# One wave of row loads, gated scalings as single steps, and operands three products ahead in a hybrid decoder layer

## The chip, the cores and the metric

One core of a Trainium2 chip runs the whole program. The metric is device microseconds of one execution. The kernel before took 892.74 us (median of 3 runs, 892.26 to 893.94). Engines are named as in the profile: PE is TensorE, DVE is VectorE, ACT is ScalarE, POOL is GpSimd, SP is SyncE, which issues most transfers.

## What is computed

One decoder layer on x of 1024 positions by 1024 features, then a final RMSNorm. All head groups and the gate come from one projection of the normed x; there are four heads of gated linear attention (GLA), four of HGRN2 and four of attention to a memory of 256 rows. Each head's output is normed, gated by Silu, and multiplied by the output weights.

```python
h = rms_norm(x, norm_w[layer])
proj = jnp.einsum('bsd,de->bse', h, w_in[layer])
(gq, gk, gv, glr, hq, hf, hi, xq, gate) = jnp.split(proj, split_idx, axis=-1)
...
mixed = jnp.concatenate([gla_o, hgrn_o, xo], axis=-1).astype(dtype)
mixed = mixed * jax.nn.silu(gate)
x = x + jnp.einsum('bse,ed->bsd', mixed, w_out[layer]).astype(dtype)
...
return rms_norm(x, final_norm_w)
```

## The kernel before

**Products.** Float32 products are made as three matmuls of float32r halves (`mm3`, L1520 to L1522: hi by hi, hi by lo, lo by hi). An operand is split by a cast on ACT (L176 for tiles, L1269 for weights: `whi`) and a subtraction of the cast on DVE or POOL (L177, L1270: `wlo`). The projections use a scheme of seven block products in place of eight (`pair`), whose operands A11, A12, S1, S2, S3, S4 and A22 are halves of x^T or sums and differences of them; some weight operands are differences too (L1262). x^T is stored as two halves along the sequence, of eight tiles of 128x512 each (`A` tiles).

**Weights ahead.** `w(i)` prepares operand i when it is asked for, and up to `LOOKAHEAD` (L1214) operands after it, as long as fewer than `NSLOT` = 5 are in use. A preparation is the difference (L1262), the cast (L1269) and the subtraction (L1270).

**Start.** `run` (L2120) loads the memory's operands, x^T half 1, weights, then 4 tiles of x's rows, then x^T half 2 (`load_x`). The program's own count of halves is 0 and 1; here they are first and second. The norm of the first half (`norm_x`, `first_half`) gives A12 and A11. The norm of the second half goes another way: its rows of x (positions on partitions) are squared on ACT with a running sum (`rows_factors`, L1386), the sums give four columns of factors (L1391, L212 to L217), and the columns are spread over all partitions by a matmul of ones with scaled identities (L232 on DVE, L233 on PE, into the PSUM tile `sc`). `second_half` (L1425 on) then scales the eight tiles (L1403) and builds S1 (L1432) and A22; `more_sums` builds S2, S3 and S4 (L1435, L1446). There are four `ml` buffers for the rows, so the second four loads (L1378) are issued after the fourth square.

**Groups.** Eight groups follow: two of memory attention (X0, X1), four of GLA (G0 to G3), two of HGRN2 (H0, H1), each two output tiles of 128 features. `emit` runs a group's projections unit by unit; `loop` goes over NB = 8 chunks of 128 positions: `step_A` (scores), `step_T`, `step_B` (state and output: PSUM tile `o` is copied by L1966 to an SBUF tile, five buffers, and squared by L1969), and after each chunk a share of the previous group's output units (`out_units`: weights by gated outputs into `pp`, L2017 adds a running sum that was loaded from DRAM, L2021 stores it). The output of four chunks (a half) is finished by `step_C`: `norm` computes the factors and scales all four blocks (`scale_o`, L1975 on ACT: one instruction of 128x256 per block in G, two of 128x128 in X and H), `gate(0)` and `gate(1)` each transpose four blocks (L982 on PE, PSUM tile `oT`), multiply by norm weight and gate (L987 on DVE), and split (L990 on ACT, L992 on POOL). The first half's three steps (`pend`) are taken in the loop, one after each chunk from the fifth on; the second half's (`self.tail`) between units of the next group's `emit`:

```python
if self.tail:
    if n in (0, 3, 5) or n > 5:
        self.tail.pop(0)()
```

X1 has no units of its own in `emit`, so X0's second half goes through `background` in X1's loop. H1's second half is finished among the last output units.

**Order.** Each engine runs its instructions in the order of its queue. A list scheduler sets that order for all engines from the program's order and its own durations, so a step moved in the source can move instructions of every queue.

## Time and profile before

| what | value |
|---|---|
| runs | 892.26, 892.74, 893.94 us, median 892.74 |
| profiled execution | 894.03 us, its span 892.3 us |
| PE busy | 856.6 us (96%) |
| DVE, ACT, POOL busy | 624.0 (70%), 529.0 (59%), 79.1 us (9%) |
| mean granted clock of TensorE | 0.99 of full |
| moved by DMA | 113.94 MB, mean 128 GB/s |

The span is the time from the first to the last instruction; 1.7 us of the execution lie around it. A matmul of 512 columns shows as 0.39 to 0.40 us busy, while the next one starts 0.23 us after it: they overlap, so the start to start distance is the cost of one. "idle before <- releaser" in a row is the time that the engine waited ahead of the instruction, and whose end released it.

### The profile page before, as it was taken

How to read it: one execution, taken by the hardware profiler on the slowest of the kernel's cores; microseconds unless marked ns; L12 is line 12 of the kernel's file. 1: busy time of each engine (PE TensorE's matmuls, PEld its weight loads, DVE VectorE, ACT ScalarE, POOL GpSimd, SP SyncE). 2: the span in 40 equal slices, each digit the busy share in tenths (PEclk: the TensorE clock that was granted, in tenths of full speed). 3: DMA queues.
4: the chain of work that ended last, by engine and by line, in shares of the span. 5: the costliest groups of instructions: out<-in, count | busy, mean ns of one | idle time of the engine just before them, and what ended most of it. 6: DMA issues, size and time to landing. Idle time of an engine off the chain costs nothing.

```text
span 892.3 us, 13841 instructions
## 1 busy us (share of the span) xinstructions
PE 856.6 (96%) x4734; PEld 714.9 (80%) x4734; DVE 624.0 (70%) x1504; ACT 529.0 (59%) x1281; POOL 79.1 (9%) x105
## 2 busy tenths in 40 slices
PE   8969999999999999999999999999999999999994
PEld 7538887889888798889888898888977788877873
DVE  5899653577558775788558865887585777666676
ACT  4637868977536754567436844576952358842373
POOL 0000112221000200011000200011000011000011
PEclk9989999999999999999999999999999999999997
DMA  9701112541136422462136422472113551044764
GB/s 327 288 11 43 53 52 75 193 164 46 50 118 213 154 71 71 154 230 78 48 119 204 162 72 71 154 233 84 38 60 119 196 182 36 25 129 131 247 228 177
DMA packets 62272, 113.94 MB, mean 128 GB/s; under 512 B 7088, under 2 KB 7216, under 8 KB 62192
## 3 DMA queue, kind: packets, MB, share of 16 engines
q1 hardware_dynamic: 61904, 112.68, 38.3%
q8 instruction: 39, 0.64, 0.3%
q14 instruction: 41, 0.34, 0.1%
q10 hardware_dynamic: 288, 0.28, 0.1%
HBM read 79.38 MB, written 33.55 MB: 127 GB/s over the span
## 4 chain that ended last, share of the span: by engine, by line
PE 80%; DVE 10%; DMA 4%; ACT 3%; issue 1%; SPq 0%; DVEq 0%; ACTq 0%
PE pp L1520 17%; PE pp L1521 17%; PE pp L1522 17%; DMA acc<-sum 3%; DVE acc L2017 2%; PE sc L1520 2%; PE sc L1522 2%; PE sc L1521 2%; PE o L1520 2%; PE o L1521 1%; PE o L1522 1%; PE o L1924 1%; PE kv L1520 1%; PE kv L1522 1%; PE kv L1521 1%
## 5 line engine op out<-in xcount | busy, mean ns | idle before, releaser
L1269 ACT CAST whi<-wst 128x512 fp32r<-128x512 f32 x193 | 117.1, 619 | 185.2 <-PE pp L1521 123.4
L1520 PE MATMUL pp<-A,whi 128*128 128x512 f32 x508 | 203.8, 403 | 9.1 <-ACT A L176 7.6
L1521 PE MATMUL pp<-A,whi 128*128 128x512 f32 x508 | 203.0, 400 | 1.0 <-DVE A L177 1.0
L1522 PE MATMUL pp<-A,wlo 128*128 128x512 f32 x508 | 201.7, 397 | 0.7 <-DVE wlo L1270 0.7
L1270 DVE TENSOR_TENSOR wlo<-wst,whi 128x512 fp32r<-128x512 f32 x193 | 131.5, 688 | 79.2 <-ACT whi L1269 74.3
L1520 PEld LDWEIGHTS pp<-A,whi 128*128 128x128 f32 x508 | 95.8, 189 | 33.6 <-ACT A L176 9.2
L1521 PEld LDWEIGHTS pp<-A,whi 128*128 128x128 f32 x508 | 96.2, 189 | 24.9 <-DVE A L177 3.0
L1522 PEld LDWEIGHTS pp<-A,wlo 128*128 128x128 f32 x508 | 96.0, 189 | 24.4 <-DVE wlo L1270 1.6
L1520 PE MATMUL pp<-whi,mh 128*128 128x512 f32 (+1 forms) x258 | 104.8, 407 | 0.3 <-DVE acc L2017 0.3
L1521 PE MATMUL pp<-wlo,mh 128*128 128x512 f32 (+1 forms) x258 | 103.0, 399 | 0.0
L1522 PE MATMUL pp<-whi,ml 128*128 128x512 f32 (+1 forms) x258 | 102.1, 396 | 0.6 <-POOL ml L992 0.6
L2017 DVE TENSOR_TENSOR acc<-acc,pp 128x512 f32<-128x512 f32 x112 | 76.6, 684 | 33.7 <-PE pp L1522 22.3
L992 POOL TENSOR_TENSOR ml<-h,mh 128x512 fp32r<-128x512 f32 x30 | 40.7, 1357 | 337.6 <-ACT mh L990 337.6
L1262 DVE TENSOR_TENSOR wst<-wst 128x512 f32<-128x512 f32 x82 | 57.8, 706 | 1.6
L1522 PEld LDWEIGHTS pp<-whi,ml 128*128 128x128 f32 x258 | 48.6, 188 | 10.9 <-POOL ml L992 1.0
L1521 PEld LDWEIGHTS pp<-wlo,mh 128*128 128x128 f32 x258 | 48.7, 189 | 8.2 <-DVE wlo L1270 0.3
L1520 PEld LDWEIGHTS pp<-whi,mh 128*128 128x128 f32 x258 | 48.6, 188 | 8.2 <-DVE acc L2017 0.4
L1975 ACT ACTIVATE o<-o,rs_r 128x128 f32<-128x128 f32 (+1 forms) x96 | 34.2, 428 | 9.3 <-DVE rs_r L195 7.8
L177 POOL TENSOR_TENSOR qk<-qk 128x128 fp32r<-128x128 f32 x28 | 13.0, 470 | 294.3 <-ACT qk L176 272.0
L990 ACT CAST mh<-h 128x512 fp32r<-128x512 f32 x32 | 19.8, 618 | 23.7 <-DVE h L987 23.5
L1969 ACT ACTIVATE junk<-o 128x128 bf16<-128x128 f32 (+1 forms) x96 | 32.6, 342 | 1.1
L1966 ACT COPY o<-o 128x256 f32<-128x256 f32 x64 | 23.6, 368 | 15.1 <-PE o L1938 4.7
(280 smaller groups left out, 1841.0 us busy)
## 6 DMA issues: line engine op xcount, KB each, us to landing
wst<-w_dram SPq DMA_DIRECT2D x128, 256.0 KB, 2.6
sum<-acc SPq DMA_DIRECT2D x112, 256.0 KB, 2.1
acc<-sum SPq DMA_DIRECT2D x96, 256.0 KB, 2.8
A<-w_dram SPq DMA_DIRECT2D x16, 256.0 KB, 6.2
A<-xT_dram SPq DMA_DIRECT2D x16, 256.0 KB, 5.3
acc<-x_dram SPq DMA_DIRECT2D x16, 256.0 KB, 2.8
A<-sum SPq DMA_DIRECT2D x16, 256.0 KB, 4.0
out_dram<-A SPq DMA_DIRECT2D x15, 256.0 KB, 2.0
```

What stands on the lines that cost most here:

```text
L990: nc.scalar.copy(hi, x)
L992: eng.tensor_tensor(lo, x, hi.bitcast(F32), op=ALU.subtract)
L1262: nc.vector.tensor_tensor(d, a, b, op=ALU.subtract)
L1269: nc.scalar.copy(hi, x)
L1270: nc.vector.tensor_tensor(lo, x, hi.bitcast(F32), op=ALU.subtract)
L1520: mm(out, lhs[0], rhs[0], start=first, stop=False, skip_group_check=skip)
L1521: mm(out, lhs[0], rhs[1], start=False, stop=False, skip_group_check=skip)
L1522: mm(out, lhs[1], rhs[0], start=False, stop=last, skip_group_check=skip)
L1966: nc.scalar.copy(osb, o)
L1969: nc.scalar.activation(junk[:, s * w : (s + 1) * w], osb[:, s], AF.Square, accum_out=g["ss"][:, c % 4, s : s + 1])
L1975: self.nc.scalar.activation(x, x, AF.Copy, scale=r)
L2017: nc.vector.tensor_tensor(dst, dst, ps, op=ALU.add)
```

## The change

The rows of x's second half come in one wave: two `qk` tiles of 128x1024 and four `ml` tiles of 128x512, all loaded ahead of x^T's second half and squared by six activations, into sums that a memset clears first. `scale_o` only collects its instructions; `step_C` gives seven steps (norm, four steps of one block, two gates). `emit` takes a step after every unit; `loop` takes one after each half of a chunk's filler units, of the tail in chunks 0 to 3 and of `pend` in chunks 4 to 7, and doesn't call `background` any more. `LOOKAHEAD` is 3.

```diff
@@ -1211,7 +1211,7 @@
 SCRATCH = 512
 NSLOT = 5
 NRAW = 5
-LOOKAHEAD = 2
+LOOKAHEAD = 3
 DRAM = bass.MemoryType.DRAM
 LN2 = 0.6931471805599453
 
@@ -1370,22 +1370,26 @@
                 nc.vector.tensor_tensor(sm, sm, sq, op=ALU.add)
         self.sm = sm
 
-    def load_rows(self, idx):
-
-        for i in idx:
-            t = self.t("ml", [P, HALF], bufs=4)
-            d = i % 2
-            self.nc.sync.dma_start(t, self.a["x"][:, 4 + i // 2, d * HALF : (d + 1) * HALF])
-            self.rows.append(t)
+    def load_rows(self):
+
+        self.rows = []
+        for b in range(4):
+            if b < 2:
+                t = self.t("qk", [P, D], bufs=4)
+                parts = [(t, 0)]
+            else:
+                parts = [(self.t("ml", [P, HALF], bufs=4), d) for d in range(2)]
+            for t, d in parts:
+                w = t.shape[-1]
+                self.nc.sync.dma_start(t, self.a["x"][:, 4 + b, d * HALF : d * HALF + w])
+                self.rows.append((t, b, d))
 
     def rows_factors(self):
         nc = self.nc
         ss = self.t("fss", [P, 4, 2])
-        for i in range(8):
-            t = self.rows[i]
-            nc.scalar.activation(t, t, AF.Square, accum_out=ss[:, i // 2, i % 2 : i % 2 + 1])
-            if i == 3:
-                self.load_rows(range(4, 8))
+        nc.vector.memset(ss, 0.0)
+        for t, b, d in self.rows:
+            nc.scalar.activation(t, t, AF.Square, accum_out=ss[:, b, d : d + 1])
         self.col = self.t("rs_r", [P, 8])
         t = self.t("rs_t", [P, 8])
         nc.vector.tensor_reduce(t[:, :4], ss, axis=AX.X, op=ALU.add)
@@ -1972,7 +1976,26 @@
         g["o"][c % 4] = osb
 
     def scale_o(self, x, r):
-        self.nc.scalar.activation(x, x, AF.Copy, scale=r)
+        self.scales.append(lambda: self.nc.scalar.activation(x, x, AF.Copy, scale=r))
+
+    def step_C(self, g, half):
+
+        norm, *gates = super().step_C(g, half)
+        mine = []
+
+        def first():
+            self.scales = mine
+            norm()
+
+        def block(b):
+            def f():
+                n = len(mine) // (4 - b)
+                for _ in range(n):
+                    mine.pop(0)()
+
+            return f
+
+        return [first] + [block(b) for b in range(4)] + gates
 
     def eps_of(self, g):
         return EPS / QSCALE**2 if g["kind"] == "G" else EPS
@@ -2088,8 +2111,7 @@
         for n, u in enumerate(units):
             u()
             if self.tail:
-                if n in (0, 3, 5) or n > 5:
-                    self.tail.pop(0)()
+                self.tail.pop(0)()
             elif self.bg and (not H or n >= 14 and n % 2 == 0):
                 self.bg.pop(0)()
 
@@ -2098,8 +2120,8 @@
         fill = list(fill)
         per = -(-len(fill) // NB)
 
-        def filler():
-            for _ in range(per):
+        def filler(i):
+            for _ in range(per // 2):
                 if fill:
                     fill.pop(0)()
 
@@ -2112,10 +2134,12 @@
             self.step_B(g, c)
             if c == 3:
                 pend = self.step_C(g, 0)
-            filler()
-            if pend and c > 3:
-                pend.pop(0)()
-            self.background()
+            for i in range(2):
+                filler(i)
+                q = pend if c > 3 else self.tail
+                if q:
+                    q.pop(0)()
+        assert not pend and not self.tail
         self.tail = self.step_C(g, 1)
 
     def run(self):
@@ -2150,8 +2174,7 @@
         self.load_x(0, range(8))
         self.mw_mv("mv", 0, 1, 2, 3)
         self.prefetch()
-        self.rows = []
-        self.load_rows(range(4))
+        self.load_rows()
         self.load_x(1, range(8))
         for f in key:
             f()
@@ -2178,7 +2201,7 @@
             self.loop(g, fill[i])
         for i, f in enumerate(last):
             f()
-            if self.tail and (i == 0 or i >= 6):
+            if self.tail and i not in (1, 6):
                 self.tail.pop(0)()
         assert self.gcol == NFLAG and self.n_prep == len(self.ops), (self.gcol, self.n_prep, len(self.ops))
 
```

The scheduler moves many instructions with this. Two places follow, the start on three engines and the last loop on one; line numbers of the changed kernel are 4 higher for most of these lines (L1386 is L1392 there, L1391 is L1395, L1403 is L1407, L1520 to L1522 are L1524 to L1526, L1936 is L1940, L1938 is L1942).

ACT in the start: the squares of the rows (into `fss`), the factors of the second half (L212, L213) and the casts of A12 and A11 (L176). Before:

```order
L1386 ACTIVATE ml,fss<-ml 128x512 x4
L1269 CAST whi<-wst 128x512
L176 CAST A<-A 128x512 x6
L1386 ACTIVATE ml,fss<-ml 128x512
L176 CAST A<-A 128x512
L1386 ACTIVATE ml,fss<-ml 128x512
L176 CAST A<-A 128x512
L1386 ACTIVATE ml,fss<-ml 128x512 x2
L1269 CAST whi<-wst 128x512
L212 ACTIVATE rs_t<-rs_t,eps 128x4
```

With the change:

```order
L1392 ACTIVATE qk,fss<-qk 128x1024 x2
L1392 ACTIVATE ml,fss<-ml 128x512 x2
L1269 CAST whi<-wst 128x512
L1392 ACTIVATE ml,fss<-ml 128x512 x2
L212 ACTIVATE rs_t<-rs_t,eps 128x4
L213 ACTIVATE rs_r<-rs_t 128x4
L176 CAST A<-A 128x512 x5
L1269 CAST whi<-wst 128x512
```

The squares and both factor activations now stand ahead of all casts of A.

PE in the start: the memory's values (L1495, L1499 with the change), q0's products and the spread L233. Before, with matmuls left out that are like those shown:

```order
L1495 MATMUL kv<-A,mh 128x512
L1520 MATMUL pp<-A,whi 128x512 x2
L1521 MATMUL pp<-A,whi 128x512
...
L1522 MATMUL pp<-A,wlo 128x512
L233 MATMUL sc<-h,ones 128x512
L1520 MATMUL pp<-A,whi 128x512 x2
L1521 MATMUL pp<-A,whi 128x512
L1522 MATMUL pp<-A,wlo 128x512
```

With the change:

```order
L1499 MATMUL o<-A,mh 128x512
L1499 MATMUL kv<-A,mh 128x512
L233 MATMUL sc<-h,ones 128x512
L1524 MATMUL pp<-A,whi 128x512
L1525 MATMUL pp<-A,whi 128x512
L1526 MATMUL pp<-A,wlo 128x512
```

The spread has moved from behind q0's 48 matmuls on A12 and A11 to ahead of them.

DVE in the start: reduction, factors (L214 to L217), scaled identities (L232), scalings of the second half (L1403, L1407), and the subtractions of the split of A12 and A11 (L177). Before, the eight L177 stand ahead of this piece:

```order
L177 TENSOR_TENSOR A<-A 128x512 x8
L1391 TENSOR_REDUCE rs_t<-fss 128x4
L1270 TENSOR_TENSOR wlo<-wst,whi 128x512 x2
L214 TENSOR_SCALAR rs_t<-rs_t 128x4
L1262 TENSOR_TENSOR wst<-wst 128x512
L215 TENSOR_TENSOR rs_t<-rs_t,rs_r 128x4
L1262 TENSOR_TENSOR wst<-wst 128x512
L216 TENSOR_TENSOR rs_t<-rs_t,rs_r 128x4
L217 SCALAR_TENSOR_TENSOR rs_r<-rs_t,rs_r 128x4
L232 TENSOR_SCALAR h<-ident,rs_r 128x128 x4
L1403 SCALAR_TENSOR_TENSOR A<-A,vec,sc 128x512 x8
L1432 TENSOR_TENSOR h<-A 128x512 x2
```

With the change:

```order
L1395 TENSOR_REDUCE rs_t<-fss 128x4
L214 TENSOR_SCALAR rs_t<-rs_t 128x4
L215 TENSOR_TENSOR rs_t<-rs_t,rs_r 128x4
L216 TENSOR_TENSOR rs_t<-rs_t,rs_r 128x4
L217 SCALAR_TENSOR_TENSOR rs_r<-rs_t,rs_r 128x4
L232 TENSOR_SCALAR h<-ident,rs_r 128x128 x4
L177 TENSOR_TENSOR A<-A 128x512 x2
L1407 SCALAR_TENSOR_TENSOR A<-A,vec,sc 128x512
L177 TENSOR_TENSOR A<-A 128x512
L1407 SCALAR_TENSOR_TENSOR A<-A,vec,sc 128x512
```

The factors stand together, and six of the eight subtractions alternate with the scalings.

PE in the loop of the last group, H1 (chunks 6 and 7): `pp` are H0's output units, `sc`, `kv` and `o` are H1's own scores, state and output, and the L982 are the transposes of the two gates of H1's first half. Before:

```order
L982 MATMUL oT<-ident,o 128x128 x4
L825 MATMUL sc<-qk 64x128
L826 MATMUL sc<-qk 64x64
...
L1947 MATMUL kv<-v,kT 128x128 x2
L1520 MATMUL pp<-whi,mh 128x512
L1521 MATMUL pp<-wlo,mh 128x512
L1522 MATMUL pp<-whi,ml 128x512
...
L982 MATMUL oT<-ident,o 128x128 x4
L1520 MATMUL pp<-whi,mh 128x512
L1936 MATMUL o<-v,scm_149 128x128
L1938 MATMUL o<-S,qk 128x128
```

With the change:

```order
L1526 MATMUL pp<-whi,ml 128x512
L982 MATMUL oT<-ident,o 128x128 x4
L1524 MATMUL pp<-whi,mh 128x512
L1525 MATMUL pp<-wlo,mh 128x512
L1526 MATMUL pp<-whi,ml 128x512
L1524 MATMUL pp<-whi,mh 128x512
L1525 MATMUL pp<-wlo,mh 128x512
L1526 MATMUL pp<-whi,ml 128x512
L982 MATMUL oT<-ident,o 128x128 x4
L1524 MATMUL pp<-whi,mh 128x512
L1940 MATMUL o<-v,scm_149 128x128
L1942 MATMUL o<-S,qk 128x128
```

Before, the scores, the state and twelve `pp` matmuls lay between the transposes of the two gates; now those come ahead of the first gate, and six `pp` matmuls lie between the gates. At the ends of the G groups the gates of the first half now also lie six `pp` matmuls apart, where there were the scores, three `kv` and twelve `pp` before.

## Rows read from the trace of the kernel before

**Rows 1.** Windows: busy time of each engine in five stretches, granted clock, DMA

```profile
core 0: us, PE busy (x) PEld busy (x) DVE busy (x) ACT busy (x) POOL busy (x), PEclk, DMA share, GB/s
22.30:36.60 14.30, 14.30 (x38) 6.64 (x38) 11.67 (x24) 7.04 (x18) 0.00 (x0) 1.00 1.03 381
36.60:66.00 29.40, 20.76 (x78) 14.54 (x77) 25.93 (x51) 13.98 (x34) 0.92 (x2) 0.88 0.11 41
48.00:55.00 7.00, 0.73 (x2) 0.00 (x0) 6.23 (x10) 1.03 (x3) 0.46 (x1) 0.79 0.00 0
66.00:75.00 9.00, 9.00 (x40) 7.23 (x39) 8.99 (x18) 5.96 (x12) 0.00 (x0) 1.00 0.01 2
140.00:200.00 60.00, 58.08 (x336) 47.88 (x335) 34.80 (x93) 53.41 (x176) 16.92 (x26) 1.00 0.46 152
```

**Rows 2.** TensorE's waits over the whole span: total, times, longest

```profile
PE pp L1520 <- ACT A L176: 7.6, 2, 6.7
PE oT L982 <- ACT o L1975: 3.2, 5, 1.6
PE o L1521 <- DVE qk L177: 1.7, 4, 0.9
PE o L1936 <- ACT o L1966: 1.6, 1, 1.6
...
PE o L1520 <- ACT o L1966: 1.2, 1, 1.2
```

**Rows 3.** Timeline of ScalarE, 22 to 44 us: start, duration, instruction, idle before

```profile
22.83 0.26 ACT L212 ACTIVATE rs_r<-pp,eps 128x4 f32<-128x4 f32 x1 [3.64 <-PE pp L224]
...
34.77 0.62 ACT L1269 CAST whi<-wst 128x512 fp32r<-128x512 f32 x1 [3.18 <-DVE wst L1262]
...
41.84 0.18 ACT L1386 ACTIVATION_READ_ACCUMULATOR ml<-ml 128x1 f32 x1
```

**Rows 4.** Timeline of VectorE, 22 to 30 and 40 to 60 us

```profile
23.36 0.16 DVE L214 TENSOR_SCALAR rs_r<-pp 128x4 f32<-128x4 f32 x1 [2.80 <-ACT rs_r L213]
...
26.37 4.04 DVE L1403 SCALAR_TENSOR_TENSOR A<-A,vec,sc 128x512 f32<-128x512 f32 x6 [1.35 <-PE sc L233]
...
42.05 0.16 DVE L1391 TENSOR_REDUCE rs_t<-fss 128x4 f32<-128x8 f32 x1 [0.54 <-ACT ml L1386]
...
48.77 5.36 DVE L1403 SCALAR_TENSOR_TENSOR A<-A,vec,sc 128x512 f32<-128x512 f32 x8 [1.93 <-PE sc L233]
54.04 1.29 DVE L1432 TENSOR_TENSOR h<-A 128x512 f32<-128x512 f32 x2
```

**Rows 5.** Timeline of TensorE, 34 to 66 us

```profile
36.07 1.03 PE L1520 MATMUL pp<-A,whi 128*128 128x512 f32 x2
...
47.71 1.02 PE L233 MATMUL sc<-h,ones 128*128 128x512 f32 x2
55.43 1.22 PE L1520 MATMUL pp<-A,whi 128*128 128x512 f32 x2 [6.70 <-ACT A L176]
...
57.60 0.63 PE L1521 MATMUL pp<-A,whi 128*128 128x512 f32 x1
58.03 0.63 PE L1520 MATMUL pp<-A,whi 128*128 128x512 f32 x1
...
65.23 0.50 PE L1521 MATMUL pp<-A,whi 128*128 128x512 f32 x1 [1.02 <-DVE A L177]
```

**Rows 6.** Timeline of TensorE at the end of G0

```profile
305.97 0.33 PE L982 MATMUL oT<-ident,o 128*128 128x128 f32 x1 [1.63 <-ACT o L1975]
```

**Rows 7.** Timeline of ScalarE at the end of G3 and in H1's loop

```profile
597.00 0.62 ACT L1269 CAST whi<-wst 128x512 fp32r<-128x512 f32 x1 [0.99 <-DVE wst L1262]
...
851.83 0.62 ACT L990 CAST mh<-h 128x512 fp32r<-128x512 f32 x1 [2.05 <-DVE h L987]
```

**Rows 8.** Timeline of VectorE in H1's loop, an output unit's add

```profile
856.36 0.69 DVE L2017 TENSOR_TENSOR acc<-acc,pp 128x512 f32<-128x512 f32 x1 [1.01 <-DMA acc<-sum]
```

**Rows 9.** Timeline of ScalarE in X0's loop

```profile
141.21 1.28 ACT L1833 ACT_TABLE_LOAD   x1
142.50 0.60 ACT L1833 ACTIVATE sg<-pp 128x512 f32<-128x512 f32 x1
```

## The prediction

> **What bounds the kernel now.** I read the windows first [rows 1], then who TensorE waits for [rows 2], then the timelines of the places where it waits [rows 3 to 9]. In [rows 1] the reader is to see that TensorE is full in a normal stretch (66 to 75 us: 9.00 of 9.00) and that one stage is not: 0.73 of 7.00 us busy at 48 to 55, with the granted clock falling to a mean of 0.79 (of two levels, 2.4 and 1.2 GHz). [Rows 2] name the waits: 7.6 us on the casts of L176, nearly all of it one wait of 6.7; the other four, 3.2, 1.7, 1.6 and 1.2, are at the ends of groups and make 7.7. The rest of the span is matmuls back to back, and the last stretch (final norm and stores) is untouched. So a change can gain only in these two kinds of places.
>
> **Part 1, the rows of x's second half.** What sets the stage is a chain: squares of the rows on ScalarE, four small steps, the spread matmul L233, then VectorE's eight scalings L1403. The last four squares wait for the second wave of rows and stand among the casts of A; the last is read out at 41.84 to 42.02 [rows 3]. The factors follow at 42.05 on VectorE, but two subtractions L1262 and two L1270 lie among them, and the scalings only start at 48.77 [rows 4], since TensorE has the spread behind all 48 matmuls of q0 (36.07 to 47.71, [rows 5]); they end at 54.13. TensorE gets its next operand at 55.43 and is fed by VectorE until 65.23, its last wait there.
>
> The change loads all rows in one wave, puts the six activations ahead of the casts of A, and the spread ahead of q0, as the order shows. I rebuild the lane step by step. The last two squares follow a weight's cast that waits for VectorE and starts at 34.77 [rows 3], by when all rows are there (their last tile would land about 33.3): 34.77 + 3 x 0.62 = 36.6. The reduction starts as soon as the last readout ends (42.05 before) and takes 0.16; with the way to the next engine I count 0.3: 36.9. The first half's same chain needed 0.53 from L212 to L214 (22.83 [rows 3] to 23.36) and from there 3.01 to the first scaling (26.37, [rows 4]): 40.5 instead of 48.77. Now six subtractions L177 alternate with the scalings: 8 x 0.67 (5.36 for eight) + 6 x 0.61 (two L1432 of the same size take 1.29 in [rows 4], and one alone 0.69) = 9.0, so the scalings end at 49.5 instead of 54.13. From there the subtraction that ends the last wait was 11.1 us later before (65.23 less 54.13); now 19 instructions at 0.61, which is 11.6 with two L1270 more and two L1446 fewer. So TensorE's last wait ends at 61.1 instead of 65.2: 4.1 gained. A second count bounds it: VectorE is idle for only 29.4 - 25.9 = 3.5 us between 36.6 and 66 [rows 1], and with the two L1262 moved behind the stage 1.2 more leaves the lane, while the new chain idles some 1.2 of its own: 3.5. **I take -4.0**, the lane weighing more. Ends: -5 if the two L1262 and the L1446 find room for nothing; 0 if the spread comes late.
>
> What it costs: q0's first matmul now stands behind the spread and moves from 36.07 to about 40.0. This is hidden, since the stage ends by VectorE's lane: q0's 48 matmuls at the pitch of 0.234 in [rows 5] take 11.2 and end at 51.2, while S1's first operands come at about 52.3. If that cover were gone it would cost up to 3.9. The two activations of 1024 replace four of 512, each at 0.62; the worst is the same columns, and nothing less is claimed. Loads: x's second half lands four tiles later; its last tile landed with the 16 tiles that share a full queue (DMA share 1.03 at 22.3 to 36.6, [rows 1]), at 0.65 each 2.6 us later, some 38.5, still ahead of the scalings at 40.5. The added memset is one small instruction of VectorE ahead of the wait for the squares: nothing.
>
> The gap ahead of q0 is the risk. Before, the clock went to 1.2 GHz inside the idle stretch after 48.73, and the matmuls after it had a pitch of 0.43 (57.60 to 58.03, [rows 5]) and beyond: a mean of 0.88 over 36.6 to 66 is 7 us at the lower level, and 48 to 55 holds only 2.9 of them [rows 1]. The new gap, from 36.6 to the spread at 39.1 and from there to 40.0, is shorter than that. If the clock falls all the same, it is rival 6.
>
> **Parts 2 and 3, the ends of groups.** Single-block steps spread four (or eight) scalings over the queue of ScalarE, and the transposes come later on TensorE. The waits of [rows 2] split like this. oT on L1975, 3.2 us, of which 1.63 at 305.97 [rows 6]: the transposes of the second half now stand behind some 30 more matmuls of 256 columns there, 3.5 us at half of 0.234 each, so most goes: -2.0. o on the subtraction L177, 1.7: that subtraction is now behind the gate's L987, but its matmuls stand later too: -1.0. o on the copy L1966, 1.6 and 1.2: in [rows 7] a copy stands behind the gate's cast at 851.83 that waited 2.05 for VectorE, and at 597 one stands behind the weight's cast that waited 0.99 for L1262. The weights are prepared one product earlier, and the two gates lie six matmuls apart, so half goes: -1.5. **Sum -4.5 of 7.7**; the ends are -7 and +1, since what is removed uncovers what is late next, as in [rows 2], where five different waits share a few ends. Looking three ahead also needs slots: five exist, four are in use at once, so no new wait by count.
>
> **The cross-attention loops.** From 140 to 200 ScalarE is busy for 53.41 of 60 [rows 1], and each switch between Silu and Exp is a table load of 1.28 us [rows 9]. The new order has two loads fewer, but in one chunk of the second loop it puts a Silu between the two Exps that one product waits for: two loads and an activation of 0.6 behind each other are 3.2 late, of which some 2 would show. **I take +1.0**, between -2.6 (two loads saved, all on the path) and +2.2. The trace shows the load and nothing besides: it starts at 141.21 and the activation behind it at 142.50. By the Trainium skill, "ScalarE: Activation LUTs", section "What ACT_TABLE_LOAD costs", a switch also pays a drain of 1.38, 2.66 in all; by that price the ends here would be -5.3 and about +4, but no row here shows the drain, so the measurement decides.
>
> **Sum.** -4.0 - 4.5 + 1.0 = -7.5, against the profiled execution of 894.03 (span 892.3 and 1.7 around it). That execution lies 1.3 above the median of the runs, 892.74; the differences carry over, and I give **885.2**.
>
> **Rivals.**
> 1. The stage keeps its length. For it: VectorE is busy 8.99 of 9.00 at 66 to 75 [rows 1], so what leaves the lane comes back right behind it. Against: two L1262 are all that is put off. Then -0.5 - 4.5 + 1.0 = -4.0: 888.7.
> 2. The ends of groups trade one wait for another. For: the scheduler only reorders, and each end has several late things. Against: the longest wait, at 305.97, has 3.5 us more cover. Then -4.0 + 0 + 1.0 = -3.0: 889.7.
> 3. Slower: an add pulled between the gates. In VectorE's new order one add L2017, which waits for a sum's transfer, stands between the two L987 at every end of a group, and behind it the second gate, the subtractions L177 and so TensorE's o. Such an add waited 1.01 for its transfer at 856.36 [rows 8]. The slack is about 0.8 us. If it is late by 2 everywhere, each of six ends loses 1.2, like the longest wait of o on the copy but one [rows 2], and it decides as soon as the six lose 0.5 each: -3.0 + 7.2 = +4.2: 897.
> 4. The change doesn't do what it says: rows land no earlier where it counts, so the spread is late, and the steps come out of the scheduler in places that cover nothing. Then 0 to +1: 893.2.
> 5. All of it works, the table loads included: -4.5 - 7.0 - 1.5 = -13: 880.
> 6. The clock falls in the gap ahead of q0. For: it fell in the gap of 6.7. Against: the new gap is half as long. Some 3.5 us at a pitch of 0.43 hold 8 matmuls instead of 15: q0 ends 1.6 later, at 52.8, at most all of it behind VectorE's lane: -2.4 - 4.5 + 1.0 = -5.9: 886.8. By the Trainium skill, "TensorE: Matmul & The Clock Gate", section "Why this matters for your kernels", idle gaps between bursts of matmuls are what costs the full clock, and by it this rival is what happens; the trace bears the rule out for the long gap, and shows no gap of the new one's length.
>
> **How the numbers follow.** About 0.2%, 1.8 us, is what a measurement of this kernel can tell from no change. Forecast 0.54 (881.5 to 888.3), and rival 6, inside its span, 0.08; rival 1 0.11, rival 2 0.12, rival 3 0.04, rival 4 0.05, rival 5 0.06. The range of 880 to 890.5 takes in the forecast and rival 6, most of rivals 1 and 2 and half of rival 5, some 0.83; it leaves out 3, 4 and the tails. Faster: 0.54 + 0.08 + 0.11 + 0.12 + 0.06, less 0.03 for the slow edges of 1 and 2, is 0.88; same 0.08; slower 0.04.
>
> **What would show it.** Right: the first scaling at 40 to 41, TensorE's last wait of the stage near 61, no wait of 6.7 us but one of 2 to 4 ahead of q0; oT on the scalings below 1.5 us in all; the copies' 2.8 halved. Wrong: a granted clock of 0.5 in q0; last wait of the stage after 64; new waits of TensorE on L987, or of the adds L2017 on their transfers at the ends of groups; sc waiting over 2 us on Exp.

## The result, and the profile after

| | runs (us) | median |
|---|---|---|
| before | 891.97 to 893.94, 5 runs | 892.72 |
| changed | 895.61 to 901.62, 5 runs | 898.80 |

The ratio is 1.0065 (95% interval 1.0046 to 1.0085): slower by some 6 us, where 7.5 us faster was forecast. Medians and ratios here and below leave out single executions that took far longer than the rest (934 us and more). The changed kernel's profiled execution took 895.61 us (span 893.9), the fastest of the five, so its trace shows least of what costs.

The windows of the changed kernel, the same stretches and columns as [rows 1]:

```profile
22.30:36.60 14.30, 13.76 (x32) 5.76 (x31) 11.35 (x24) 8.38 (x20) 0.00 (x0) 1.00 1.05 403
36.60:66.00 29.40, 24.75 (x94) 17.86 (x95) 28.04 (x52) 14.52 (x30) 15.11 (x1) 0.94 0.08 29
48.00:55.00 7.00, 6.74 (x31) 5.16 (x29) 7.00 (x12) 4.11 (x10) 4.11 (x1) 1.00 0.10 37
66.00:75.00 9.00, 9.00 (x40) 7.21 (x40) 9.00 (x20) 7.23 (x14) 6.05 (x2) 1.00 0.00 0
140.00:200.00 60.00, 55.75 (x324) 45.84 (x324) 32.20 (x86) 49.65 (x167) 15.93 (x24) 1.00 0.46 148
```

TensorE's worst stretch is gone (6.74 of 7.00 busy at 48 to 55), and 36.6 to 66 holds 24.75 us of its work in place of 20.76. But the loops of cross-attention, 140 to 200, hold 55.75 in place of 58.08, with ScalarE less busy than before.

TensorE's waits in the changed kernel answer to [rows 2]:

```profile
PE pp L1525 <- DVE A L177: 2.6, 3, 1.0
PE sc L233 <- DVE h L232: 2.5, 1, 2.5
PE pp L1738 <- DVE acc L2040: 2.2, 3, 0.9
PE o L1525 <- DVE qk L177: 1.9, 5, 0.7
PE pp L1524 <- DVE acc L2040: 1.8, 1, 1.8
PE oT L982 <- DVE h L987: 1.8, 4, 1.1
PE pp L1524 <- DVE sg L1803: 1.6, 1, 1.6
...
PE o L1940 <- ACT o L1970: 0.4, 1, 0.4
```

The wait of 6.7 us is gone, oT's wait for the scalings has no row any more, and o's waits for the copies are 0.4 in place of 2.8. In their place stand new ones: 2.2 and 1.8 us behind VectorE's adds L2040 (L2017 before), 1.8 behind L987, 1.6 behind the gate's tiles (`sg`).

The start in the changed kernel, on VectorE ([rows 4] before) and TensorE ([rows 5]):

```profile
36.09 0.16 DVE L1395 TENSOR_REDUCE rs_t<-fss 128x4 f32<-128x8 f32 x1 [0.54 <-ACT ml L1392]
36.85 0.17 DVE L214 TENSOR_SCALAR rs_t<-rs_t 128x4 f32<-128x4 f32 x1 [0.60 <-ACT rs_r L213]
...
40.69 0.75 DVE L1407 SCALAR_TENSOR_TENSOR A<-A,vec,sc 128x512 f32<-128x512 f32 x1 [0.97 <-PE sc L233]
...
48.39 1.40 DVE L1407 SCALAR_TENSOR_TENSOR A<-A,vec,sc 128x512 f32<-128x512 f32 x2
```

```profile
38.58 2.08 PE L233 MATMUL sc<-h,ones 128*128 128x512 f32 x2 [2.52 <-DVE h L232]
39.66 1.42 PE L1524 MATMUL pp<-A,whi 128*128 128x512 f32 x1
...
61.28 0.50 PE L1525 MATMUL pp<-A,whi 128*128 128x512 f32 x1 [1.02 <-DVE A L177]
...
81.62 0.50 PE L1524 MATMUL pp<-A,whi 128*128 128x512 f32 x1 [1.08 <-ACT sg L1837]
```

Reduction at 36.09, first scaling at 40.69, scalings done at 49.79 (48.39 + 1.40), q0's first matmul at 39.66, the last wait on VectorE's split at 61.28. A wait of 1.08 at 81.62 is new.

What the adds waited for, VectorE's waits over the whole span, before and then changed:

```profile
DVE acc L2017 <- PE pp L1522: 22.3, 26, 4.5
...
DVE acc L2017 <- DMA acc<-sum: 7.5, 10, 1.3
...
DVE acc L2017 <- DMA acc<-x_dram: 3.4, 3, 1.4
```

```profile
DVE acc L2040 <- DMA acc<-sum: 19.2, 20, 3.1
...
DVE acc L2040 <- PE pp L1526: 16.4, 17, 6.6
...
DVE acc L2040 <- DMA acc<-x_dram: 8.2, 4, 3.1
```

Before, the adds waited mostly for TensorE (22.3 us), which costs TensorE nothing; 10.9 us were waits for a load (7.5 and 3.4). Now 27.4 us are (19.2 and 8.2). The total alone is no price, as the experiments will show. Two places show what such a wait does. In X1's loop, on VectorE and on TensorE:

```profile
171.86 1.28 DVE L2040 TENSOR_TENSOR acc<-acc,pp 128x512 f32<-128x512 f32 x2 [2.93 <-DMA acc<-x_dram]
```

```profile
172.61 0.50 PE L1524 MATMUL pp<-whi,mh 128*128 128x512 f32 x1 [1.84 <-DVE acc L2040]
```

At the end of G1, on VectorE and on TensorE:

```profile
393.35 0.69 DVE L2040 TENSOR_TENSOR acc<-acc,pp 128x512 f32<-128x512 f32 x1 [2.63 <-DMA acc<-sum]
...
398.14 0.74 DVE L987 SCALAR_TENSOR_TENSOR h<-oT,vec,sg 128x512 f32<-128x512 f32 x1
398.96 0.69 DVE L2040 TENSOR_TENSOR acc<-acc,pp 128x512 f32<-128x512 f32 x1
399.63 0.75 DVE L987 SCALAR_TENSOR_TENSOR h<-oT,vec,sg 128x512 f32<-128x512 f32 x1
...
403.92 0.69 DVE L2040 TENSOR_TENSOR acc<-acc,pp 128x512 f32<-128x512 f32 x1 [0.82 <-DMA acc<-sum]
```

```profile
398.94 0.66 PE L982 MATMUL oT<-ident,o 128*128 128x128 f32 x4 [1.12 <-DVE h L987]
...
404.66 0.50 PE L1738 MATMUL pp<-aux,wup 128*128 128x512 f32 x1 [0.89 <-DVE acc L2040]
```

An add waits 2.63 us for its load, everything on VectorE behind it is late, the first gate's L987 starts at 398.14, and the second gate's transposes wait 1.12 for it. Then another add waits 0.82, and L1738 waits 0.89 for that add, since it needs the PSUM tile that the add empties. The load behind the 2.63 us was issued at 387.83, as soon as the store that held its buffer had landed, and landed at 393.22: 5.4 us, where the mean load of the sum in this execution took 3.0. The kernel before has such a load there too (4.4 us, issued at 388), but its adds wait for TensorE at that time (1.49 us at 392.32) and not for the load.

### The profile page after: what moved, and what is told of

Its sections match the earlier page's. It is cut to its first block, busy times and chain, and to the rows that moved or that the text cites. A ratio compares the mean times of both kernels' runs of the same rounds, so it can differ in the third digit from the quotient of the medians.

```text
span 893.9 us, 13844 instructions
## 1 busy us (share of the span) xinstructions
PE 859.4 (96%) x4734; PEld 714.9 (80%) x4734; DVE 619.8 (69%) x1505; ACT 526.6 (59%) x1275; POOL 98.9 (11%) x105
## 4 chain that ended last, share of the span: by engine, by line
PE 65%; DVE 14%; DMA 10%; ACT 7%; issue 3%; SPq 0%; DVEq 0%; ACTq 0%
PE pp L1524 15%; PE pp L1525 15%; PE pp L1526 15%; DMA acc<-sum 5%; DMA sum<-acc 3%; DVE acc L2040 2%; DVE wlo L1270 2%; ACT L1759 2%; PE o L1928 1%; DMA acc<-x_dram 1%; PE oT L982 1%; DVE A L1407 1%; PE o L1524 1%; PE o L1525 1%; ACT whi L1269 1%
## 5 line engine op out<-in xcount | busy, mean ns | idle before, releaser
L1269 ACT CAST whi<-wst 128x512 fp32r<-128x512 f32 x193 | 118.1, 619 | 189.8 <-PE pp L1525 132.0
L1524 PE MATMUL pp<-A,whi 128*128 128x512 f32 x508 | 203.3, 402 | 4.2 <-DVE sg L1803 1.6
L1526 PE MATMUL pp<-A,wlo 128*128 128x512 f32 x508 | 201.7, 397 | 0.6 <-DVE wlo L1270 0.6
L1270 DVE TENSOR_TENSOR wlo<-wst,whi 128x512 fp32r<-128x512 f32 x193 | 135.2, 705 | 85.4 <-ACT whi L1269 81.2
L1524 PEld LDWEIGHTS pp<-A,whi 128*128 128x128 f32 x508 | 95.8, 189 | 28.6 <-DVE acc L1551 2.3
L1526 PEld LDWEIGHTS pp<-A,wlo 128*128 128x128 f32 x508 | 95.8, 189 | 24.4 <-DVE wlo L1270 1.5
L2040 DVE TENSOR_TENSOR acc<-acc,pp 128x512 f32<-128x512 f32 x112 | 76.5, 684 | 49.2 <-DMA acc<-sum 19.2
L1524 PE MATMUL pp<-whi,mh 128*128 128x512 f32 (+1 forms) x258 | 105.8, 410 | 2.0 <-DVE acc L2040 1.8
L1526 PE MATMUL pp<-whi,ml 128*128 128x512 f32 (+1 forms) x258 | 102.1, 396 | 0.0
L1524 PEld LDWEIGHTS pp<-whi,mh 128*128 128x128 f32 x258 | 48.6, 188 | 11.5 <-DVE acc L2040 3.5
L1526 PEld LDWEIGHTS pp<-whi,ml 128*128 128x128 f32 x258 | 48.5, 188 | 10.2
L177 POOL TENSOR_TENSOR wup<-qk,wup 128x128 fp32r<-128x128 f32 x32 | 35.8, 1136 | 122.4 <-ACT wup L176 88.4
L177 POOL TENSOR_TENSOR qk<-qk 128x128 fp32r<-128x128 f32 x28 | 13.2, 476 | 285.6 <-ACT qk L176 266.5
```

The costliest lines, as they stand in the source:

```text
L177: eng.tensor_tensor(to[1], x, to[0].bitcast(F32), op=ALU.subtract)
L1269: nc.scalar.copy(hi, x)
L1270: nc.vector.tensor_tensor(lo, x, hi.bitcast(F32), op=ALU.subtract)
L1524: mm(out, lhs[0], rhs[0], start=first, stop=False, skip_group_check=skip)
L1526: mm(out, lhs[1], rhs[0], start=False, stop=last, skip_group_check=skip)
L2040: nc.vector.tensor_tensor(dst, dst, ps, op=ALU.add)
```

## The experiments

**One part at a time.** The change has three parts that can be taken alone: rows in one wave; steps of one block and their places; `LOOKAHEAD`. The edits are the hunks of the change that belong to each, and in the fourth kernel only

```diff
-LOOKAHEAD = 3
+LOOKAHEAD = 2
```

Expected of the rows alone:

> The kernel before with the rows in one wave alone. Theory (the start gives about 2 us, as the changed kernel's trace shows: its last wait of the stage at 61.3 instead of 65.2, with 1.2 given back at 81.6): ratio 0.996 to 0.999, 889 to 892 us, spread of the runs as before (about 2 us). Rival (the one wave of rows itself costs, through the queue order behind it): 1.000 or above.

Of the steps alone:

> The kernel before with the single-block steps alone (rows in two waves, operands two ahead). Theory (the steps put output units where their adds wait for the transfer of the running sum): ratio 1.005 to 1.011, 897 to 902 us, and the runs several us apart; VectorE's waits of the output adds on transfers go from 7.5 us to 15 or more. Rival (looking three ahead is what costs): ratio 0.993 to 1.000, waits on transfers as before.

Of three ahead alone:

> The kernel before with operands prepared three ahead alone. Theory (the steps cost, not this): within 0.3% of before, 890 to 895 us. Rival (three ahead puts casts and subtractions ahead of urgent work and weight loads ahead of sums in the queue): 896 to 902 us, with the waits on transfers raised.

Of rows and steps with two ahead:

> The changed kernel with operands two ahead again. Theory (the steps cost): 896 to 901 us, like the changed kernel within 2 us. Rival (three ahead costs): 885 to 890 us.

| kernel | median us | ratio to before, 95% |
|---|---|---|
| rows alone | 891.33 | 0.9972 (0.9960 to 0.9984) |
| steps alone | 893.56 | 1.0003 (0.9990 to 1.0016) |
| three ahead alone | 903.08 | 1.0098 (1.0082 to 1.0115) |
| rows and steps, two ahead | 890.25 | 0.9963 (0.9951 to 0.9976) |
| all three (the change) | 898.80 | 1.0065 (1.0046 to 1.0085) |

The theory that the steps cost fell: the whole loss is `LOOKAHEAD`, some 9 us on the kernel before and 9 on rows and steps. Without it the change is 3.3 us faster than before. The waits that the theory asked for did come: the adds waited for loads for 23.3 us with the steps alone (11.5 for the sum, 11.8 for x), 24.1 in rows and steps, 19.8 with three ahead alone, 9.6 with the rows alone. So rows and steps waits more than twice as long for loads as the kernel before, and is faster.

To see where, I added up the columns of all matmuls in order of time and took the time at which each kernel had done the same share of them, less the time of the kernel before (one profiled execution each, so a microsecond or two of a start may be chance):

| up to about | rows | steps | three ahead | rows and steps | the change |
|---|---|---|---|---|---|
| 104 us, the start | -2.7 | +1.6 | +1.6 | -2.0 | -2.4 |
| 228 us, cross-attention | -3.0 | +5.7 | +2.7 | +2.1 | +0.5 |
| 565 us, most of GLA | -3.3 | +2.7 | +2.3 | -1.2 | +3.5 |
| 879 us, HGRN2 and end | -5.1 | +0.8 | +9.4 | -2.9 | +2.4 |

The steps lose some 4 us in the cross-attention loops and give about 5 back at the ends of groups. Three ahead on the kernel before loses at the starts of H0 and H1, two times 2.1, and at the ends of groups; on top of rows and steps it loses 6.3 us in the GLA groups, where TensorE's waits go from 1.0 us to 5.2. The start's +1.6 in two columns is the clock: in those two executions 55 to 62 us ran at a mean of 0.50 and 0.51, before at 0.72.

**The rows' part seen alone.** In the kernel with the rows alone TensorE's waits at the ends of groups stay as in [rows 2]:

```profile
PE oT L982 <- ACT o L1979: 3.1, 5, 1.5
...
PE o L1524 <- ACT o L1970: 0.9, 2, 0.5
PE o L1940 <- ACT o L1970: 0.8, 1, 0.8
```

so what removed them is the steps.

**Is it a burst?** Output units hold four of the five slots until the last of them. The call behind that unit prepares two operands at once before, three with `LOOKAHEAD` 3. Two edits were meant to take the burst away: at most two preparations when a new operand is asked for,

```diff
-        while self.n_prep < min(i + 1 + LOOKAHEAD, len(self.ops)) and self.live < NSLOT:
+        if i != self.at:
+            self.at, self.top = i, self.n_prep + (2 if i else NSLOT)
+        while self.n_prep < min(i + 1 + LOOKAHEAD, len(self.ops), self.top) and self.live < NSLOT:
```

or the first two output weights released after unit 11, their last use, and one operand prepared in unit 12 and in unit 14:

```diff
-                if n == 2 * NB - 1 and c1 == HALF:
-                    for i in range(4):
-                        self.w_done(base + i)
+                if last:
+                    done = range(4) if n == 2 * NB - 1 and c1 == HALF else ()
+                else:
+                    done = {11: (0, 1), 15: (2, 3)}.get(n, ())
+                    if n in (12, 14) and self.n_prep < len(self.ops) and self.live < NSLOT:
+                        self.prepare(self.n_prep)
+                        self.prefetch()
+                for i in done:
+                    self.w_done(base + i)
```

The changed kernel with the first edit:

> The changed kernel, but at most two operands are prepared when a new operand is asked for, so that the call behind a group's last output unit (which frees four of five slots) prepares two as before and the third one product later. Theory (looking three ahead costs by the burst of three preparations at the ends of groups): 889 to 893 us, as with two ahead. Rival (it costs by the order all through, at HGRN2's first products above all): 896 to 901 us.

The kernel before with three ahead and the first edit:

> The kernel before with three ahead, and at most two preparations for a new operand. Theory (the burst): 891 to 896 us. Rival (the order all through): 900 to 904 us, with TensorE's two waits on a weight's cast, 3.1 us, still at the start of H0 and H1.

The changed kernel with the second:

> The changed kernel with the first two output weights' slots released after unit 11, where they were last used, and one operand prepared at unit 12 and at unit 14, so that only one is left for the call behind the group. Theory (the burst): 886 to 892 us. Rival (the order all through): 896 us or more; a third possibility is that the preparations in units 12 to 14 meet the gates' work there and give back what they save.

Rows and steps, two ahead, with the second:

> Rows and steps with two ahead, and the same early release. Theory (the ends of groups are bound by the burst of two preparations too): 886 to 889 us. Rival (two are hidden): 889 to 893 us.

| kernel | median us | ratio to before, 95% |
|---|---|---|
| the change, two at most | 899.06 | 1.0067 (1.0044 to 1.0090) |
| three ahead alone, two at most | 901.89 | 1.0103 (1.0077 to 1.0129) |
| the change, early release | 898.15 | 1.0058 (1.0035 to 1.0080) |
| rows and steps, early release | 890.31 | 0.9970 (0.9957 to 0.9983) |

None of the four moved beyond its interval from its kernel without the edit. But this doesn't exclude the burst, since the edits hardly reached the queues: the scheduler put back what they had moved in the program's order. I compared the traces engine by engine, as sequences of operations and tiles, and count as moved what lies outside the longest order that both share. The first edit moves nothing at all in the kernel before with three ahead, on any engine, so 901.89 and 903.08 are two measurements of one order. The second moves 3 instructions on ScalarE and 2 on VectorE, in either kernel, and no matmul. Only the changed kernel with the first edit has another order (18 matmuls, 12 instructions on ScalarE and 33 on VectorE moved), and it took as long as without. Whether a burst costs stays open.

**Without the running sum.** The adds' waits for loads had doubled, so I took the running sum out: no load, no store, and each unit's result only copied. These kernels leave out the sum of the groups' output products, and only the last group's reaches the output.

```diff
-                nc.sync.dma_start(t, self.a["x"][:, b, h * HALF : (h + 1) * HALF] if src is None else src)
+                if last:
+                    nc.sync.dma_start(t, self.a["x"][:, b, h * HALF : (h + 1) * HALF])
...
-                nc.vector.tensor_tensor(dst, dst, ps, op=ALU.add)
-                if not last:
...
-                    nc.sync.dma_start(self.sums[h, b], dst)
+                if last:
+                    nc.vector.tensor_tensor(dst, dst, ps, op=ALU.add)
+                else:
+                    nc.vector.tensor_scalar(dst, ps, 1.0, None, op0=ALU.mult)
```

The kernel before:

> The kernel before without the running sum of the output products: no loads and stores of it, each unit's result is only copied out of PSUM (only the last group's product reaches the output). It gives the base for the next three. Both theories: 885 to 893 us, since TensorE waits for few of these transfers.

With three ahead:

> The same without the running sum, operands three ahead. Theory (three ahead costs through the order on ScalarE and VectorE, whatever the transfers do): still 6 us or more above the kernel before without the sum. Rival (it costs because its sums come later; the mean transfer of a sum took 2.78 us against 2.66): within 2 us of it.

With rows and steps:

> Rows and steps, two ahead, without the running sum. Theory (the steps' cost in the cross-attention loops, some 4 us in the trace, is adds that wait for transfers): 5 us or more below the kernel before without the sum. Rival (it is order): 2 to 4 us below it, as with the sum.

The changed kernel:

> The changed kernel without the running sum. Theory (three ahead costs through the order): 5 us or more above rows and steps with two ahead without the sum. Rival (through the sums' transfers): within 2 us of it.

| kernel | with the sum, ratio | without it, ratio (95%) | without it, us | the sum costs |
|---|---|---|---|---|
| before | 1 | 0.9940 (0.9918 to 0.9962) | 887.19 | 0.6% |
| three ahead | 1.0098 | 0.9996 (0.9983 to 1.0009) | 893.07 | 1.0% |
| rows and steps | 0.9963 | 0.9844 (0.9819 to 0.9869) | 878.62 | 1.2% |
| the change | 1.0065 | 0.9875 (0.9848 to 0.9902) | 881.61 | 1.9% |

Without the sum the whole change is 5.6 us faster than before (881.61 against 887.19), and rows and steps 8.6. With it the change is 6 slower: the sum costs some 6 us before and 17 in the changed kernel. Three ahead costs 5.9 us without the sum on the kernel before (893.07 less 887.19) and 3.0 on rows and steps (881.61 less 878.62), where it costs 9 with it, so neither theory of the pair is right alone. A copy takes VectorE as long as an add (687 and 684 ns on the mean, in the kernel before without and with the sum), so that is not the difference. But the edit takes out more than transfers: the order moves with it. Rows and steps with the sum and without it differ in 80 matmuls, 66 instructions on ScalarE and 102 on VectorE, where `LOOKAHEAD` moves 52, 60 and 139. So this table prices the sum together with the order that goes with it; a comparison within one order follows under the buffers.

A cost of order alone shows in the kernel before with three ahead, at H0's first products. ScalarE, then TensorE:

```profile
648.45 0.60 ACT L1269 CAST whi<-wst 128x512 fp32r<-128x512 f32 x1
649.07 1.28 ACT L1756 ACT_TABLE_LOAD   x1
650.36 0.51 ACT L1756 ACTIVATE qk<-qk,ln 128x256 f32<-128x256 f32 x1
650.89 1.28 ACT L1755 ACT_TABLE_LOAD   x1
652.18 0.42 ACT L1755 ACTIVATE qk<-aux 128x256 f32<-128x256 f32 x1
652.62 1.28 ACT L1756 ACT_TABLE_LOAD   x1
653.91 0.51 ACT L1756 ACTIVATE qk<-qk,ln 128x256 f32<-128x256 f32 x1
654.33 0.60 ACT L1269 CAST whi<-wst 128x512 fp32r<-128x512 f32 x1
```

```profile
654.98 0.50 PE L1520 MATMUL pp<-A,whi 128*128 128x512 f32 x1 [1.57 <-ACT whi L1269]
```

Three activations of 0.4 to 0.5 us, each behind a table load of 1.28 of its own, stand between two casts, and the second cast (654.33) is the one that the next product needs. Over 612 to 700 this kernel has 16 table loads, the one before 14, rows and steps 13. TensorE waits on a weight's cast twice, 3.1 us in all, the second time at H1's first products, and without the sum the same two waits take 3.2. In the changed kernel there is one load more than in rows and steps there, and 0.8 us are lost.

**More buffers for the sum.** A load of the sum takes one of three buffers, and waits until the store of the unit three before has landed. Is that reuse what makes the adds wait? Room for more buffers came first from a slot of the prepared operands (`NSLOT` 4, with the early release, two ahead):

```diff
-NSLOT = 5
+NSLOT = 4
...
-                t = acc[h, b] = self.a_tile(F32) if last else self.t("acc", [P, HALF], bufs=3)
+                t = acc[h, b] = self.a_tile(F32) if last else self.t("acc", [P, HALF], bufs=5)
...
-                fetch(n + (6 if last else 2))
+                fetch(n + (6 if last else 4))
```

The control with four slots alone:

> Rows and steps with two ahead and the early release of the first two output weights, and four slots in place of five; the control for the next two. Theory (the waits for sums decide, the weights' lead does not): 889 to 893 us, like the early release with five slots. Rival (a slot less makes weights late at the ends of groups): 895 us or more.

With four buffers:

> The same with the freed room given to the running sum: four buffers for it in place of three, and its loads issued one unit earlier. Theory (an add waits because its load waits for the store of the unit three before): 884 to 888 us, and VectorE's waits of the adds on transfers fall from 24 us to under 12. Rival (the transfers themselves are slow, by what else moves): no change from the control.

With five:

> The same with five buffers and loads two units earlier. Theory: 880 to 885 us, near the 878.6 of the kernel without any sum. Rival: no change from the control.

The control took 897.37 us (ratio 1.0043, 1.0025 to 1.0061), four buffers 899.37 (1.0067, 1.0045 to 1.0090), five 892.39 (0.9997, 0.9980 to 1.0013). The control already missed: a slot less costs 7 us. Four buffers missed too: the adds' waits for loads fell from the control's 25.6 us to 10.8, and the time did not fall. The control is no clean one, though, since the fourth buffer moves 69 matmuls, 81 instructions on ScalarE and 113 on VectorE. Between four and five buffers nothing moves on these three engines; only loads are issued one unit earlier, on SyncE. So this is the clean step: one more buffer, in one order, gains 7.0 us (899.37 to 892.39, and no run of either lies among the other's). In the trace of five buffers, VectorE's waits of the adds, then TensorE's wait on weights:

```profile
DVE acc L2040 <- DMA acc<-sum: 4.2, 3, 2.7
```

```profile
PE pp L1524 <- ACT whi L1269: 5.7, 4, 2.2
```

The adds' waits are down to 4.2 us, and up to 565 us this trace is 0.2 us behind that of rows and steps without any sum, where rows and steps with the sum is 7.2 behind and the change 11.9. It then loses 13 us up to the end, where rows and steps loses 4. TensorE's 5.7 us of waits for casts are part of that, and the control has the same 5.7, so they belong to the missing slot.

So the room was taken from the raw weight tiles instead:

```diff
-NRAW = 5
+NRAW = 4
```

The control:

> Rows and steps with two ahead, all five slots, and four raw weight tiles in place of five: the control for the next two. Theory (raw tiles are early enough): 889 to 893 us. Rival (weights come late): 895 us or more.

With four buffers for the sum:

> The same with the freed room as a fourth buffer of the running sum, its loads one unit earlier. Theory (the reuse of three buffers is what makes the adds wait, 7 us by the trace up to the end of the GLA groups): 883 to 887 us and ahead of the control by 3 us or more, the adds' waits on transfers under 12 us. Rival (the order is what decides): within 2 us of the control.

The changed kernel, three ahead, with the same:

> The changed kernel, three ahead, with four raw tiles and four buffers of the running sum. Theory (two thirds of what three ahead costs goes through the sums): 2 to 5 us above two ahead with the same buffers. Rival: still 8 to 10 us above it.

The control took 893.23 us (1.0003, 0.9987 to 1.0018), four buffers 890.89 (0.9969, 0.9954 to 0.9984), and three ahead with four buffers 896.49 (1.0031, 1.0018 to 1.0043). The adds' waits on loads, rows and steps with three buffers and then the kernel with four:

```profile
DVE acc L2040 <- DMA acc<-sum: 15.4, 17, 3.2
...
DVE acc L2040 <- DMA acc<-x_dram: 8.7, 5, 2.8
```

```profile
DVE acc L2040 <- DMA acc<-sum: 4.8, 5, 1.7
...
DVE acc L2040 <- DMA acc<-x_dram: 2.8, 2, 2.0
```

24.1 us of waits (26.7 in the control) became 7.6, and the gain on the control is 2.3 us, under the 3 that the theory asked for. In the trace four buffers lose 4.3 us in the start against rows and steps, and gain as much behind it. The control loses 1.9 of these 4.3 too; the rest comes with a lower granted clock (a mean of 0.64 at 42 to 48 us, 1.00 in the control). Three ahead now costs 5.6 us where it cost 9. How much of the difference is the buffer is not shown, since the fourth buffer moves the order here as well (80, 66 and 102 from its control), and no kernel has three ahead, four raw tiles and three buffers.

These last kernels allow the comparison that the one without the sum lacked. Behind the start (113 us on), the kernel with four raw tiles and four buffers and rows and steps without the sum have one order, except for one matmul and one instruction of VectorE; so have their two partners with three ahead. The time from there to the last matmul, one profiled execution each, in us:

| | no sum | sum, four buffers | the sum costs |
|---|---|---|---|
| two ahead | 754.9 | 761.2 | 6.3 |
| three ahead | 755.8 | 767.6 | 11.8 |
| three ahead costs | 0.9 | 6.4 | |

So in one and the same order three ahead costs 0.9 us when no sum is moved and 6.4 when it is (one execution each, the last of them 1.7 us over its median). There TensorE's wait of the transposes for L987 is 0.8 us without the sum and 5.5 with it. So in these kernels what three ahead costs goes mostly through the sum's transfers. No version with the sum in place was clearly better than rows and steps with two ahead, 890.25 us, which beats both kernels.

## Why the prediction was wrong

Point by point, with the steps as the prediction put them.

**Part 1 held in its steps, and less in its sum.** First scaling at 40.69 (forecast 40.5), scalings done at 49.79 (49.5), last wait at 61.28 (61.1), q0's first matmul at 39.66 (40.0). By 61 us the 4 were there; 1.1 went back at 81.62, where TensorE waits for ScalarE (L1837, a gate's activation). The rows alone and rows and steps don't have this wait; there TensorE waits 0.9 us for a weight's cast (L1269) at 74.50 and 75.25, and 1.6 us of the gain are gone by 81 us. So rival 1's outcome holds in part, by ScalarE's queue and not by VectorE's as it was argued. Alone the part gave 0.28%, 2.5 us, against 4.0.

**The ends of groups came out near the working with two ahead.** From 228 us to the end, steps alone gain 4.9 us in the trace (5.7 down to 0.8), rows and steps 5.0; forecast was 4.5, though part of that was to come from preparing one product earlier, which these kernels don't do. oT's wait for the scalings went from 3.2 to nothing, the copies' from 2.8 to 0.4; o's wait for the subtraction stayed (1.7, now 1.9), and 1.8 us behind L987 are new.

**The cross-attention loops were mis-sized.** +1.0, with the ends -2.6 and +2.2, came out at some +4 in the trace for steps with two ahead. The working looked at ScalarE's table loads, and had these right: 6 of them at 140 to 200 us against 8. Rows and steps still loses here. Without the sum these loops lose next to nothing (-2.7 us ahead of them, -2.4 behind them, against the kernel before without it). In rows and steps TensorE waits 2.2 us here behind adds, as at 172.61 in the changed kernel, and in the kernel with four buffers, which has the order of the one without the sum here, neither this wait nor the loss is there. So adds that wait for loads are about half of it by the rows; the order changed too, and the rest is not assigned.

**The step that failed** is the one on looking three ahead: "five exist, four are in use at once, so no new wait by count". It costed `LOOKAHEAD` at nothing, and even counted it on the side of the gain. It costs 9 us, measured twice. The count of slots says when an operand may be prepared; it says nothing of what each preparation moves on VectorE, ScalarE and in the queue of transfers, which all run in order. From 7.5 us faster to 6.1 slower is 13.6 us: some 9 are this step, some 3 the cross-attention loops and 1.5 the start.

**Rival 3 had the kind of mechanism**, an add that waits for its transfer with the gate's work queued behind it on VectorE, but not the place. The add between the two gates of G1 (398.96, between L987 at 398.14 and 399.63) didn't wait; those that did stand ahead of both gates (393.35), behind both (403.92) and in the cross-attention loops. So its 897 lies near the 898.80 by luck. It was given 0.04, because the sum's transfers were judged by one row, 1.01 us at 856.36, when adds waited 10.9 us for loads in all, and 22.3 for TensorE. Where TensorE comes earlier, a wait for it can become a wait for the load. The total is no measure of the cost either: 24.1 us in rows and steps, which is faster, and 27.4 in the change, which is slower. What counts is which of these waits TensorE gets to feel. That the change doesn't do what it says (rival 4) is refuted by the start.

**The clock.** Rows alone and rows and steps run the same order through this stage on VectorE, ScalarE and TensorE, and yet it fell behind the gap ahead of q0 in one execution and not in the other. 36 to 42 us, rows and steps and then the rows alone:

```profile
36.00:42.00 6.00, 3.48 (x9) 2.37 (x9) 5.06 (x15) 3.24 (x9) 0.00 (x0) 0.81 0.35 125
```

```profile
36.00:42.00 6.00, 3.48 (x13) 1.96 (x12) 4.70 (x15) 3.62 (x9) 0.00 (x0) 1.00 0.40 142
```

So rival 6 happens in some executions, the changed kernel's among them. The Trainium skill, "TensorE: Matmul & The Clock Gate", section "Why this matters for your kernels", names idle gaps between bursts of matmuls as what drops the clock; these two rows show one gap, 2.52 us ahead of the spread, with either outcome. It costs about 1 us, and is not hidden behind VectorE's lane as the prediction has it. With q0 slower, a weight's cast waits longer for a product of q0, the cast of A behind it is late, and so is VectorE. Rows and steps on ScalarE and VectorE, then the rows alone on ScalarE:

```profile
44.17 0.62 ACT L1269 CAST whi<-wst 128x512 fp32r<-128x512 f32 x1 [4.67 <-PE pp L1525]
...
45.34 0.69 DVE L177 TENSOR_TENSOR A<-A 128x512 fp32r<-128x512 f32 x1 [0.98 <-ACT A L176]
```

```profile
43.42 0.62 ACT L1269 CAST whi<-wst 128x512 fp32r<-128x512 f32 x1 [3.55 <-PE pp L1525]
```

With the rows alone VectorE has no such wait. In the changed kernel the spread itself is slow (two matmuls in 2.08 us), and VectorE's first scaling waits 0.97 for it, as the row at 40.69 shows.

**What stays open.** That the step failed, and by how much, is shown; why three ahead makes TensorE wait on the sum's transfers is not. The burst is not tested. The reuse of buffers costs (7.0 us between four and five), but its share of the 9 us is not isolated. On the kernel before, where 5.9 of the 9 stay without the sum, order at HGRN2's start is some of it. The sum's stores also take longer in the changed kernel (a mean of 2.64 us from issue to landing against 2.41 in rows and steps; the loads 3.01 against 2.99), and no run tells whether that is cause or effect.

## What to carry to other kernels

Before costing an earlier or tighter order, look at what the engines that run in order would wait for next: a wait for TensorE can hide a wait for a transfer behind it, so read more than the longest row, and then ask which of the waits reaches the engine that decides. Preparing further ahead is not free when buffers allow it: the count of slots leaves out what it moves in the queues. Try each part of a change by itself, since here one number took back what two others had gained. And where a scheduler sets the order, compare the queues of the two traces before reading an experiment: one edit here moved nothing and so tested nothing, and leaving the sum out moved as much as the edit under test.

## What was not expected of the hardware

Behind the same gap of about 2.5 us the granted clock fell in one execution and held in another (0.81 against 1.00 above), and the fall reached TensorE by way of two other engines. Stores of the sum took longer with more buffers: in the kernels with four slots a mean of 2.55 us from issue to landing with three buffers, 2.98 with four, 3.12 with five, while the loads took 3.04, 3.02 and 3.17. And runs without the sum lie closer together: the kernel before 0.5 us apart in 4 runs without it, where 13 runs with it beside them lie 5.8 apart; three ahead 1.6 us in 10 runs, where 5 runs with the sum lie 3.7 apart.
